# One diffusion block on one core: each engine's instructions ordered by the framework's timeline simulation

## The chip, the cores and the metric

The kernel runs on one core of one Trainium2 chip. The metric is device time of one execution in microseconds (us); less is better. A core has five engines, each with a queue of its own: TensorE (PE) does matmuls and transposes, VectorE (DVE), ScalarE (ACT) and GpSimd (POOL) do elementwise work, and SyncE (SP) issues the DMA transfers of the weights.

## The reference

One layer of a diffusion backbone over 256 latent tokens, with 256 context tokens that only give keys and values. D is 2048, the feed-forward width 8192, all in float32:

```python
mod_l = jnp.split(silu_c @ w_mod[l] + b_mod[l], 6, axis=-1)
mod_c = jnp.split(silu_cc @ w_mod[l] + b_mod[l], 6, axis=-1)
hl = modulate(rms_norm(xl, norm1_g[l]), mod_l[0], mod_l[1])
hc = modulate(rms_norm(xc, norm1_g[l]), mod_c[0], mod_c[1])
zl = hl @ w_in[l] + b_in[l]                       # conv a | sgu u,v | q,k,v | 3 gates
zkv = hc @ w_in[l, :, K_OFF:G_OFF] + b_in[l, K_OFF:G_OFF]
y_na_l = neighbourhood_attention(q, k, v, kc, vc, na_rpb[l])
y_conv = conv_branch(z[..., :2 * CONV_DIM], ...)  # gate, 31 taps over tokens, layer norm, silu, projection
y_sgu = sgu_branch(z[..., 2 * CONV_DIM:Q_OFF], ...)
y_att = y_na @ w_na_out
xl = xl + mod_l[2][:, None, :] * ((g_conv * y_conv + g_sgu * y_sgu + g_att * y_att) @ w_o + b_o)
hl2 = modulate(rms_norm(xl, norm2_g[l]), mod_l[3], mod_l[4])
xl = xl + mod_l[5][:, None, :] * (jnp.square(jax.nn.relu(hl2 @ w1 + b1)) @ w2 + b2)
return rms_norm(xl, final_g)
```

## The kernel before

**Weights.** All weights are streamed once, in tiles of 512 KB (128 x 1024 float32), named raw0, raw1, ... in the order of their loads. `Stream.fetch` issues each load on SP (line 84) into one of 8 buffers. A tile that feeds a matmul is split into a rounded part and a rest: whi on ACT (line 90) and wlo on DVE (line 91), 4 buffers of each. A product is then three matmuls of the parts: lines 172 and 173 with the weights stationary (512 and 256 columns), or lines 178, 179 and 180 with the activations stationary (512 columns each). They accumulate in 4 PSUM banks ("acc"); 4 more ("aux") serve transposes, the modulation products and attention.

**Start and key/value blocks.** The rows of D are worked through in five blocks. For each block, `mod_block` multiplies the conditioning vectors with the tiles of `w_mod` on PE (line 314, "gemv"). These tiles are not split, and the four column groups of the array take one row group each:

```python
                for r in range(rt):
                    g = r0 + r
                    q = g % 4
                    PE.matmul(gb[j][32 * q : 32 * q + 32, :cols], lhsT=cst[:, g], rhs=raw[:, r],
                              start=g < 4, stop=g >= NK - 4, tile_position=(0, 32 * q))
```

Its result is copied by ACT (ge, line 332), transposed by PE (gp, line 335) and reduced by DVE (gv, line 336) to a scale and a shift (m1A, m1B). `rows` then transposes the normalized tokens on PE (hT, line 349) and makes h, the input of all projections, in parts: ACT line 356, DVE lines 358 and 359. `kv_block` multiplies h with the key and value columns of the block: banks k (evacuated by ACT, then DVE line 389, then POOL) and banks vb (DVE line 407). The tokens come from `nat` tiles, those of the context from SP at line 240.

**The other modulation vectors** (`mod_cols`) are made on DVE, one product with each half of a tile (lines 874 and 876, "ga"): two per tile of `w_mod`, 16 for a column. `col_finish` transposes such a column on PE (mcol, line 905), sums it on ACT and puts it in place on DVE (line 910). These tiles are dealt in between the weight tiles of the last key/value block, the projections and the gates.

**After that**: query projection and attention, dealt in steps among the projections of the convolution and gating branches (scores S on PE lines 528 and 529, maximum mx and exponent on DVE lines 530 and 532 and ACT, transposes pT on PE line 551, output o on PE line 562); convolution taps on DVE; the branch projections with their gates; the norm of the convolution branch (`spread`: dg on DVE line 695, crs on PE line 696); the output projection; a second norm (n on line 696, x1T transposes on line 1050); the feed-forward part with `bk` banks; and the last norm.

**Order.** The Python code is written in one sequence, with steps dealt out by small counters. The framework takes this program and puts the instructions of each engine into an order of its own, by a simple model of how long things take. Each engine then executes its list from front to back. Buffers and data dependences are what the code says; semaphore waits follow from them.

## Time and profile before

| | |
|---|---|
| runs | 1778.26, 1782.08, 1789.81 us; median 1782.08 |
| profiled execution | 1788.73 us, span 1786.9 us |
| PE / DVE / ACT / POOL busy | 97% / 75% / 48% / 8% |
| granted TensorE clock, mean | 0.994 |
| DMA | 411.86 MB, 230 GB/s over the span |

A row of a timeline gives the start of an instruction or of a run of equal ones, the time from the first start to the last end, and in brackets how long the engine was idle before it and which instruction released it. Matmuls overlap, so the distance from one start to the next tells what one costs. A list of waits adds the idle times up by what was waited for. Idle time of an engine that nothing waits for costs nothing.

### The profile page before, as it was taken

The numbers are of one execution on the slowest core, as the hardware profiler recorded it, in microseconds if no ns is written. First come the engines' busy times: TensorE is split into PE (matmuls) and PEld (weight loads), VectorE is DVE, ScalarE is ACT, GpSimd is POOL, SyncE is SP. The second block draws the span as 40 slices with busy tenths as digits, with TensorE's granted clock in tenths as the row PEclk, the third lists the DMA queues.
The fourth block names the chain that finished last, engine by engine and source line by source line (L and its number), as shares of the span: only waits on it lengthen the run. The fifth ranks groups of instructions, "written<-read, shape, count | busy, mean of one in ns | idle before, by whom it ended". The sixth has DMA issues, their size and how long they took to land.

```text
span 1786.9 us, 24042 instructions
## 1 busy us (share of the span) xinstructions
PE 1731.8 (97%) x8727; PEld 1422.4 (80%) x8727; DVE 1336.6 (75%) x2099; ACT 862.1 (48%) x1290; POOL 150.9 (8%) x193
## 2 busy tenths in 40 slices
PE   6999898999999999999999999999999999999997
PEld 3667787788888888788878878888888888888886
DVE  4656998799989977898877559746775676666664
ACT  4433345987555444554434446543453445334443
POOL 1221450321000100200010010000000000000000
PEclk9999999999999999999999999999999999999999
DMA  9787788645766668899996567757876775666552
GB/s 322 261 309 263 253 262 262 169 138 173 220 187 199 185 206 284 280 324 337 312 322 221 187 192 257 257 191 239 265 250 196 239 223 189 204 196 187 185 195 83
DMA packets 265688, 411.86 MB, mean 230 GB/s; under 512 B 13182, under 2 KB 126002, under 8 KB 265570
## 3 DMA queue, kind: packets, MB, share of 16 engines
q1 hardware_dynamic: 259410, 391.21, 67.8%
q0 software_dynamic: 5584, 18.07, 3.4%
q8 instruction: 68, 1.11, 0.3%
q10 hardware_dynamic: 576, 1.05, 0.2%
q14 instruction: 50, 0.41, 0.1%
HBM read 408.18 MB, written 2.10 MB: 230 GB/s over the span
## 4 chain that ended last, share of the span: by engine, by line
PE 61%; DVE 14%; issue 11%; DMA 10%; ACT 3%; SPq 1%; POOL 0%; DVEq 0%; POOLq 0%; ACTq 0%
PE bk L172 14%; PE bk L180 10%; PE bk L179 10%; PE bk L178 10%; DMA raw<-in_w_mod_dram 7%; PE bk L173 7%; DVE wlo L91 5%; DVE ga L876 3%; DMA raw<-in_w_in_dram 2%; PE k L172 2%; PE gemv L314 1%; ACT whi L90 1%; PE vb L178 1%; PE vb L180 1%; PE vb L179 1%
## 5 line engine op out<-in xcount | busy, mean ns | idle before, releaser
L90 ACT CAST whi<-raw 128x1024 fp32r<-128x1024 f32 x544 | 570.0, 1050 | 605.6 <-PE bk L180 388.5
L91 DVE TENSOR_TENSOR wlo<-raw,whi 128x1024 fp32r<-128x1024 f32 x544 | 672.3, 1239 | 250.6 <-ACT whi L90 248.3
L172 PE MATMUL bk<-h,whi 128*128 128x512 f32 x1536 | 545.2, 398 | 0.0
L173 PE MATMUL bk<-h,wlo 128*128 128x256 f32 x1536 | 432.0, 282 | 2.7 <-DVE wlo L91 2.5
L172 PEld LDWEIGHTS bk<-h,whi 128*128 128x128 f32 x1536 | 289.6, 189 | 71.0 <-issue 3.1
L173 PEld LDWEIGHTS bk<-h,wlo 128*128 128x128 f32 x1536 | 291.5, 190 | 5.5 <-DVE wlo L91 4.3
L876 DVE SCALAR_TENSOR_TENSOR ga<-raw,cst,ga 128x512 f32<-128x512 f32 x240 | 185.9, 776 | 73.4 <-DMA raw<-in_w_mod_dram 70.5
L179 PE MATMUL bk<-wlo,g 128*128 128x512 f32 x512 | 199.2, 389 | 0.0
L180 PE MATMUL bk<-whi,g 128*128 128x512 f32 x512 | 199.2, 389 | 0.0
L178 PE MATMUL bk<-whi,g 128*128 128x512 f32 x512 | 199.2, 389 | 0.0
L179 PE MATMUL bk<-wlo,h 128*128 128x512 f32 x448 | 175.2, 391 | 3.7 <-DVE wlo L91 3.6
L178 PE MATMUL bk<-whi,h 128*128 128x512 f32 x448 | 175.5, 392 | 0.0
L180 PE MATMUL bk<-whi,h 128*128 128x512 f32 x448 | 174.5, 390 | 0.0
L179 PEld LDWEIGHTS bk<-wlo,g 128*128 128x128 f32 x512 | 96.1, 188 | 20.0
L178 PEld LDWEIGHTS bk<-whi,g 128*128 128x128 f32 x512 | 96.1, 188 | 19.9
L180 PEld LDWEIGHTS bk<-whi,g 128*128 128x128 f32 x512 | 96.1, 188 | 19.9
L637 DVE SCALAR_TENSOR_TENSOR cT<-uT,wcT,cT 128x244 f32<-128x244 f32 (+14 forms) x240 | 107.2, 497 | 0.5
L179 PEld LDWEIGHTS bk<-wlo,h 128*128 128x128 f32 x448 | 84.1, 188 | 23.2 <-DVE wlo L91 6.3
L172 PE MATMUL k<-h,whi 128*128 128x512 f32 x256 | 94.9, 411 | 3.9 <-DVE h L359 2.8
L180 PEld LDWEIGHTS bk<-whi,h 128*128 128x128 f32 x448 | 84.1, 188 | 17.4
L178 PEld LDWEIGHTS bk<-whi,h 128*128 128x128 f32 x448 | 84.1, 188 | 17.2
L173 PE MATMUL k<-h,wlo 128*128 128x256 f32 x256 | 72.6, 285 | 0.5 <-DVE wlo L91 0.5
(267 smaller groups left out, 2075.8 us busy)
## 6 DMA issues: line engine op xcount, KB each, us to landing
raw<-in_w_ff_dram SPq DMA_DIRECT2D x256, 512.0 KB, 4.4
raw<-in_w_in_dram SPq DMA_DIRECT2D x208, 512.0 KB, 4.6
raw<-in_w_mod_dram SPq DMA_DIRECT2D x192, 512.0 KB, 5.2
raw<-in_w_o_dram SPq DMA_DIRECT2D x32, 512.0 KB, 4.4
raw<-in_w_na_out_dram SPq DMA_DIRECT2D x16, 512.0 KB, 3.7
raw<-in_w_sgu_out_dram SPq DMA_DIRECT2D x16, 512.0 KB, 5.4
raw<-in_w_conv_out_dram SPq DMA_DIRECT2D x16, 512.0 KB, 7.2
bias<-in_na_rpb_dram POOLq DMA_DIRECT2D x16, 192.0 KB, 4.8
```

The source lines that it names most:

```text
L90: nc.scalar.copy(hv, rv)
L91: nc.vector.tensor_tensor(lv, rv, hv.bitcast(F32), ALU.subtract)
L172: PE.matmul(bk, lhsT=hi[:, j, c0 : c0 + P], rhs=xhl, start=start, stop=False)
L173: PE.matmul(bk[:, T:], lhsT=lo[:, j, c0 : c0 + P], rhs=xhl[:, :T], start=False, stop=stop)
L178: PE.matmul(bk, lhsT=xh, rhs=hi, start=start, stop=False)
L179: PE.matmul(bk, lhsT=xh, rhs=lo, start=False, stop=False)
L180: PE.matmul(bk, lhsT=xl, rhs=hi, start=False, stop=stop)
L314: PE.matmul(gb[j][32 * q : 32 * q + 32, :cols], lhsT=cst[:, g], rhs=raw[:, r], start=g < 4, stop=g >= NK - 4, tile_position=(0, 32 * q))
L637: V.scalar_tensor_tensor(a[:, lo:hi], u[:, lo + d : hi + d], wj, a[:, lo:hi], ALU.mult, ALU.add)
L876: V.scalar_tensor_tensor(a[0], raw[:, r], sc, a[0], ALU.mult, ALU.add)
```

## The change

The context that the program is built in is told to order the instructions by its timeline simulation in place of its simple model:

```diff
--- before.py
+++ after.py
@@ -1205,7 +1205,7 @@
         arrays[f"in_{name}_dram"] = a
         args.append(nc.dram_tensor(f"in_{name}_dram", a.shape, mybir.dt.from_np(a.dtype), kind="ExternalInput").ap())
     args.append(nc.dram_tensor("out_0_dram", (1, T, D), F32, kind="ExternalOutput").ap())
-    with tile.TileContext(nc) as tc:
+    with tile.TileContext(nc, schedule_with_timeline_sim=True) as tc:
         tile_block(tc, *args)
     r = run_bass_kernel_spmd(nc, [arrays], core_ids=[0])
     return r.results[0]["out_0_dram"]
```

Each engine executes the same instructions as before; their order and a few waits differ. On PE 2468 of 8480 matmuls stand at another place, by at most 184 places, on DVE 1471 of 2089 instructions by at most 119, on ACT 512 by at most 21. Nearly all of them belong to the time up to some 820 us; the feed-forward part stands as it was. On SP 15 loads move, all among the first 33: the context tiles nat_23 and nat_24 go ahead of raw8 and raw9, nat_38 goes behind raw15 and nat_49 behind raw18 (before they stood ahead of raw10 and of raw12). On POOL 17 instructions move by at most 4 places. ACT and DVE follow the moved loads in the order of their first splits.

PE, the modulation product of the second key/value block (gemv_151 with raw34 to raw38; vb_155 is the last value bank of the first block). Before:

```order
L179 MATMUL vb_155_863<-wlo33_819,h_113_612 128x512
L180 MATMUL vb_155_863<-whi33_818,h_113_612 128x512
L314 MATMUL gemv_151_826<-raw34_824,cst_91 32x512 x2
L314 MATMUL gemv_151_826<-raw35_829,cst_91 32x512 x2
L314 MATMUL gemv_151_826<-raw36_833,cst_91 32x512 x2
L314 MATMUL gemv_151_826<-raw37_837,cst_91 32x512 x2
L314 MATMUL gemv_151_826<-raw38_871,cst_91 32x512 x2
L335 MATMUL gp_158_898<-ident_76,ge_157_896 128x128 x4
```

The same in the change, among the key banks k_121 to k_131 of the first block:

```order
L314 MATMUL gemv_151_826<-raw34_824,cst_91 32x512 x2
L172 MATMUL k_121_659<-h_113_612,whi23_562 128x512
L173 MATMUL k_121_659<-h_113_612,wlo23_563 128x256
L172 MATMUL k_125_677<-h_113_612,whi23_562 128x512
L173 MATMUL k_125_677<-h_113_612,wlo23_563 128x256
L314 MATMUL gemv_151_826<-raw35_829,cst_91 32x512 x2
L172 MATMUL k_127_686<-h_108_597,whi23_562 128x512
L173 MATMUL k_127_686<-h_108_597,wlo23_563 128x256
L172 MATMUL k_127_686<-h_108_597,whi23_562 128x512
L173 MATMUL k_127_686<-h_108_597,wlo23_563 128x256
L314 MATMUL gemv_151_826<-raw36_833,cst_91 32x512 x2
```

Ten matmuls that stood next to each other now stand in pairs, each pair between key matmuls.

DVE, the last key/value block (h_316 and h_321 are the last four columns of h; ga_329 and ga_365 two columns of the other modulation vectors). Before:

```order
L358 TENSOR_SCALAR hf_317_2032<-hT_315_2027,m1A_138,m1B_139 128x256
L358 TENSOR_SCALAR hf_319_2039<-hT_318_2035,m1A_138,m1B_139 128x256
L359 TENSOR_TENSOR h_316_2030<-hf_317_2032,h_316_2030 128x256
L359 TENSOR_TENSOR h_316_2030<-hf_319_2039,h_316_2030 128x256
L358 TENSOR_SCALAR hf_322_2047<-hT_320_2042,m1A_138,m1B_139 128x256
L358 TENSOR_SCALAR hf_324_2054<-hT_323_2050,m1A_138,m1B_139 128x256
L359 TENSOR_TENSOR h_321_2045<-hf_322_2047,h_321_2045 128x256
L359 TENSOR_TENSOR h_321_2045<-hf_324_2054,h_321_2045 128x256
```

The end of that piece in the change, and what follows it:

```order
L359 TENSOR_TENSOR h_321_2045<-hf_322_2047,h_321_2045 128x256
L359 TENSOR_TENSOR h_321_2045<-hf_324_2054,h_321_2045 128x256
L876 SCALAR_TENSOR_TENSOR ga_365_2404<-raw112_2402,cst_91,ga_365_2404 128x512
L876 SCALAR_TENSOR_TENSOR ga_329_2123<-raw106_2254,cst_91,ga_329_2123 128x512
L876 SCALAR_TENSOR_TENSOR ga_365_2404<-raw112_2402,cst_91,ga_365_2404 128x512
L876 SCALAR_TENSOR_TENSOR ga_365_2404<-raw113_2407,cst_91,ga_365_2404 128x512 x2
L876 SCALAR_TENSOR_TENSOR ga_365_2404<-raw116_2479,cst_91,ga_365_2404 128x512 x2
L876 SCALAR_TENSOR_TENSOR ga_365_2404<-raw117_2483,cst_91,ga_365_2404 128x512 x2
L389 TENSOR_TENSOR t_333_2158<-k_332_2149,t_333_2158 128x256
```

Products of line 876 stand between the steps that make h and ahead of them, so that these come 14 to 19 places later; the key evacuations of line 389 come after a row of products, 15 to 18 places later.

PE, the same block (mcol_378 is the transposed column ga_365, k_357 a key bank). Before:

```order
L172 MATMUL k_352_2307<-h_321_2045,whi104_2194 128x512
L173 MATMUL k_352_2307<-h_321_2045,wlo104_2195 128x256
L905 MATMUL mcol_354_2332<-ident_76,ga_329_2123 128x128 x4
L172 MATMUL k_357_2350<-h_306_1998,whi107_2260 128x512
L173 MATMUL k_357_2350<-h_306_1998,wlo107_2261 128x256
```

In the change:

```order
L172 MATMUL k_352_2307<-h_321_2045,whi104_2194 128x512
L173 MATMUL k_352_2307<-h_321_2045,wlo104_2195 128x256
L905 MATMUL mcol_378_2629<-ident_76,ga_365_2404 128x128 x4
L172 MATMUL k_357_2350<-h_306_1998,whi107_2260 128x512
L173 MATMUL k_357_2350<-h_306_1998,wlo107_2261 128x256
```

The transposes of ga_329 (mcol_354) and of the convolution weights (line 605) went up, ahead of the bank k_340, and those of ga_365, which stood 161 rows behind k_357, now stand ahead of it.

## Rows read from the trace of the kernel before

**Rows 1.** The page: busy time, share of the span, instructions of each engine.
```profile
PE 1731.8 (97%) x8727; PEld 1422.4 (80%) x8727; DVE 1336.6 (75%) x2099; ACT 862.1 (48%) x1290; POOL 150.9 (8%) x193
```
**Rows 2.** Stages: length; PE, PEld, DVE, ACT, POOL busy; clock, DMA share, GB/s.
```profile
150.00:200.00 50.00, 49.05 (x263) 38.23 (x262) 41.36 (x65) 18.41 (x35) 19.59 (x19) 1.00 0.84 285
200.00:250.00 50.00, 46.06 (x240) 38.60 (x239) 48.36 (x82) 23.65 (x54) 23.65 (x21) 0.97 0.70 224
...
300.00:350.00 50.00, 44.39 (x253) 36.10 (x253) 42.36 (x97) 46.47 (x94) 11.76 (x14) 0.97 0.64 184
...
1110.00:1700.00 590.00, 588.24 (x3003) 500.88 (x3002) 384.11 (x489) 264.23 (x332) 1.59 (x3) 1.00 0.68 217
```
**Rows 3.** Timeline of PE, 14 to 64 us: start, length, instruction, [idle before].
```profile
19.27 1.08 PE L314 MATMUL gemv<-raw,cst 128*32 128x256 f32 x8 [0.42 <-DMA raw<-in_w_mod_dram]
20.86 1.08 PE L314 MATMUL gemv<-raw,cst 128*32 128x256 f32 x8 [0.51 <-DMA raw<-in_w_mod_dram]
...
31.38 0.77 PE L172 MATMUL k<-h,whi 128*128 128x512 f32 x1 [2.79 <-DVE h L359]
```
**Rows 4.** Timeline of PE, groups of line 314 between 64 and 84 us.
```profile
74.23 1.05 PE L314 MATMUL gemv<-raw,cst 128*32 128x512 f32 x2
75.21 0.50 PE L172 MATMUL k<-h,whi 128*128 128x512 f32 x1
...
81.05 1.92 PE L314 MATMUL gemv<-raw,cst 128*32 128x512 f32 x16
82.90 0.50 PE L178 MATMUL vb<-whi,h 128*128 128x512 f32 x1
```
**Rows 5.** Timeline of PE, 206 to 238 us; eight matmuls like the second row.
```profile
206.75 0.90 PE L349 MATMUL hT<-ident,nat 128*128 128x128 f32 x6 [3.64 <-DVE gv L336]
...
207.88 0.63 PE L178 MATMUL vb<-whi,h 128*128 128x512 f32 x1
...
211.10 0.39 PE L180 MATMUL vb<-whi,h 128*128 128x512 f32 x1
...
237.38 0.60 PE L905 MATMUL mcol<-ident,ga 128*128 128x128 f32 x4
237.74 0.48 PE L172 MATMUL k<-h,whi 128*128 128x512 f32 x1
```
**Rows 6.** Timeline of DVE: the last product of raw121.
```profile
257.92 0.74 DVE L876 SCALAR_TENSOR_TENSOR ga<-raw,cst,ga 128x512 f32<-128x512 f32 x1
```
**Rows 7.** DVE's groups by line, 200 to 262 us: busy us, mean ns, idle before.
```profile
L876 DVE SCALAR_TENSOR_TENSOR ga<-raw,cst,ga 128x512 f32<-128x512 f32 x31 | 25.8, 844 | 0.7 <-DMA raw<-in_w_mod_dram 0.6
L91 DVE TENSOR_TENSOR wlo<-raw,whi 128x1024 fp32r<-128x1024 f32 x9 | 14.1, 1564 | 0.7 <-ACT whi L90 0.7
L407 DVE TENSOR_TENSOR vN<-vN,vb 128x512 f32<-128x512 f32 x10 | 6.7, 682 | 0.6 <-PE vb L180 0.6
L389 DVE TENSOR_TENSOR t<-k,t 128x256 f32<-128x256 f32 x16 | 6.5, 415 | 0.1
```
**Rows 8.** What PE waited for, 300 to 450 us: us in total, times, longest.
```profile
PE S L528 <- DVE mx L532: 3.2, 1, 3.2
PE S L529 <- ACT kl L502: 2.0, 2, 1.2
PE o L562 <- DVE mx L532: 1.7, 2, 1.5
```
**Rows 9.** Timeline of PE, late places: the two norms.
```profile
746.03 0.73 PE L696 MATMUL crs<-dg,ones 128*128 128x128 f32 x4 [2.82 <-DVE dg L695]
...
747.31 0.63 PE L180 MATMUL bk<-whi,sg 128*128 128x512 f32 x1
...
1061.63 1.19 PE L696 MATMUL n<-dg,ones 128*128 128x128 f32 x4 [3.88 <-DVE dg L695]
```

## The prediction

> **What bounds the kernel now.** I read the busy shares first, then the stages, then the waits of TensorE (PE), then the timelines of the stages that the change touches. PE is busy for 97% of the span [rows 1]; the page counts matmuls that overlap, so what can be lost or won is the time in which PE starts nothing, and that lies in stages. In the feed-forward part it is near nothing: 588.24 of 590 us are busy [rows 2], and its order stays. VectorE (DVE), 75% on average, is the second limit and a local one: from 200 to 250 us it is busy for 48.36 of 50 us, while in the 50 us before it had 8.6 us to spare [rows 2]. So in the last block of keys and values, whatever is put in front of something that PE needs makes PE late by its own length.
>
> The profiled execution took 1788.73 us (span 1786.9 and 1.8 around it), 6.65 above the median of the three runs, 1782.08. The sum is made against the profiled one and then carried over by taking 6.65 off.
>
> **The change, part by part.** No operation is added or taken away, so every price is one of place: a wait that comes, a wait that goes, and matmuls that run alone where they ran side by side.
>
> *The first loads.* The two first context tiles go ahead of raw8 and raw9, the first two weight tiles of the keys. The matrix-vector matmuls at 19.27 and 20.86 each start when a tile has landed [rows 3], so tiles of 512 KB come some 1.5 us apart, and raw8 comes 2 x 1.5 = 3 us later. PE's first key matmul waits until 31.38 for DVE's h [rows 3]; part of the 3 us falls under that wait. The other two context tiles go behind four and seven modulation tiles, 6 to 10 us later in the queue; they feed the second context rows, which PE needs at some 46 us, with the value matmuls in between as cover. If the cover holds, the price is 0; if both come out, some 5 us. I take +2.5, the middle.
>
> *The matrix-vector rounds.* Four column groups of the modulation product run side by side when their matmuls stand next to each other. A round of two matmuls takes PE from 74.23 to 75.21, 0.98 us; two full rounds of 16 take 81.05 to 82.90, 1.85, so 0.93 each [rows 4]. A round with one or two matmuls thus costs as much as one with eight. Counting neighbours in the order of before gives 43 rounds in 22 groups, in the change 48 in 26, all the extra ones of 512 columns: raw34 to raw38 become five groups among the key matmuls instead of one. Five rounds at 0.93 are 4.65 us; from below it is the two or three that can fall under an idle PE at the start, so 2 us, from above 4.65 with four more entries into a group at 0.3 each, 6 us. I take +4.5, near the full price, because most of the split rounds stand between matmuls that wait for nothing.
>
> *The last key and value block, 201 to 265 us: what goes.* PE waits 3.64 us at 206.75 for DVE's gv, and the eight matmuls after it take 0.63 us where 0.39 is usual [rows 5]: 8 x 0.24 = 1.9. In the change PE does two more value banks before those transposes, so both go: -5.5.
>
> *What comes.* DVE makes h_316 and h_321 14 to 19 places later, behind gate products of line 876, and PE must turn the second gate column, mcol_378, ahead of k_357, where before it stood 161 rows behind k_357. Its products end with raw121, in before at 257.92 + 0.74 = 258.66 [rows 6]. Of what DVE did between 206.5 and 258.7 only a little is moved behind them: 8 key evacuations of line 389, 2 splits of line 91, 3 of line 407 and three small ones, so 8 x 0.415 + 2 x 1.564 + 3 x 0.682 [rows 7] + 1.3 = 9.8 us. Since DVE is full there, the last product ends at 258.7 - 9.8 = 248.9 or so. k_357 started 237.74, right behind the 0.36 us of mcol_354 at 237.38 [rows 5]. It can now start at 248.9 + 0.4 = 249.3, which is 11.6 later; 0.9 of it is transposes that PE did later before and no longer has to. So PE leaves this block about 10.7 us behind, the 5.5 won already in it, and h_316 only moves a part of that wait to an earlier place. The splits that later blocks wait for are late by the same queue.
>
> How does that add to the 7 us of the first two parts? If DVE comes to 206 us in time, the lag at the end is the 10.7 alone, since a late PE waits less for DVE. If DVE is held up as much as PE is, it is 7 + 10.7 = 17.7. DVE had 8.6 us to spare in the 50 us before [rows 2], which speaks for the first; its tiles come through the same raw buffers that PE's lag holds, which speaks for the second. I take 13, so +6 for this block on top of the 7. From below, DVE keeps up and the block gives its 5.5 back.
>
> [...]
>
> *Attention, 297 to 450 us.* PE's scores, transposes and outputs move up to 181 places later in its order, behind projection matmuls that are ready. Three waits, S for DVE's maximum 3.2, S for the low half of the keys 2.0 and o for the maximum 1.7 [rows 8], are 6.9 us, and the slow matmuls after the 3.2 cost about as much as those at 207.88, 1.5 more. That is -8.4 if all go. Nothing is gained if DVE, 42.36 of 50 us busy there [rows 2] and now with the tail of the block before in front, is as late as the scores are; I take -8, since the moves (some 25 matmuls of 0.35 a pair and more) are longer than any of the three waits.
>
> *Late places.* The 2.82 us for crs at 746.03 goes (its transposes are 17 places later) and with it eight matmuls at 0.63 [rows 9], -4.7. Against that, up to 4.5 us of normalization now stands ahead of eleven weight splits in DVE's order at 722 to 737 us, which PE reaches about 3 us late, and one such split at 908 costs 0.7. At 1061.63 PE already waits 3.88 for dg [rows 9]; the second norm product now stands behind eight transposes (1.8 us) and three more of DVE's products come before the first h2, +2 to +3. Together +2; all bad +6, all good -4.
>
> **The sum:** 2.5 + 4.5 + 6 - 8 + 2 = +7, so 1795.7 against the profiled time, and 1789 against the median.
>
> **Rivals.**
> *The DVE queue decides, and nothing gives it back.* The mechanism is the same wait of mcol_378 and k_357, with DVE arriving at 206 us as late as PE: lag 17.7, and the backlog then reaches attention, where its waits stay (0 in place of -8). It decides from the point where DVE's 8.6 us to spare are used up by late tiles. 17.7 + 2 is +19.7, so 1802, slower by just over 1%. For it: the 48.36 of 50 and the small part that moved behind. Against it: the spare time, and attention moved far.
> *DVE keeps up.* The removed waits are real rows and the added ones are only worked out: 2.5 + 4.5 - 5.5 - 8.4 - 4 is -11, so 1771; with the cheap ends of the first two parts, 0 and 2, it is 1766. For it: the products need no PE, and a faster start of the tiles would let them run in idle DVE time. Against it: DVE has hardly any idle time at 200 to 250.
> *The order hardly matters.* PE is the full engine, and a lag in one place is a shorter wait in the next: 1782. The feed-forward half speaks for it, the list of waits against it. [...] The 48.36 of 50 us [rows 2] speaks against it for one stage.
>
> **How the numbers follow.** Forecast, 1789, a chance of 0.57; the DVE queue, 0.23; DVE keeps up, 0.12; no effect, 0.08. One per cent, about what a measurement of this kernel can tell from no change, is 17.8 us, so faster means under 1764 and slower over 1800. Faster needs the second rival with all its cheap ends, and more: 0.09. Slower takes the first rival and the upper edge of the forecast, whose bad ends (+5, +6, +6 in place of 2.5, 4.5 and 2) reach 1797: 0.25. The rest, 0.66, is within. The range, 1769 to 1806, takes in most of the second rival and of the first, a tenth left out at each end.
>
> **What would show it.** In the changed profile: the first key matmul at 33 to 34 us; more and shorter groups of line 314 between 65 and 110; no wait of the transposes for gv near 206, but waits of k for h (line 359) near 222 to 230 and of mcol for ga (line 876) near 245 to 260, together 8 to 15 us; fewer than 3 us of waits for mx, kl and pT in attention; no wait for dg near 746. A list of PE's waits without mcol or h in it would make the largest positive term wrong; waits for mx as long as before would make the largest negative one wrong. A new line in the feed-forward stage would lie outside all of this.

## The result and the profile after

The change makes the kernel slower: 1823.56 us median of 4 runs (1821.57 to 1828.80) against 1781.62 for the kernel before, a ratio of 1.0229 (95% interval 1.0206 to 1.0251). The forecast was 1789, range 1769 to 1806, with a chance of 0.25 for slower by over 1%. The profiled execution took 1821.57 us, span 1819.7, 32.8 us longer than that of before.

PE executes the same matmuls. Its busy time grew by 9.8 of these 32.8 us; the rest is time between matmuls. The page's busy row, which answers to [rows 1]:

```profile
PE 1741.6 (96%) x8727; PEld 1426.9 (78%) x8727; DVE 1328.4 (73%) x2099; ACT 862.0 (47%) x1290; POOL 149.5 (8%) x193
```

Two of the stages, with the columns of [rows 2]. From 200 to 250 us PE is busy for 40.00 us in place of 46.06, and the granted clock is 0.90 in place of 0.97; DVE is as full as before:

```profile
200.00:250.00 50.00, 40.00 (x198) 33.01 (x198) 48.51 (x82) 15.62 (x34) 14.82 (x15) 0.90 0.83 262
...
300.00:350.00 50.00, 46.05 (x261) 38.87 (x260) 43.29 (x89) 36.51 (x72) 5.15 (x6) 0.97 0.73 225
```

What PE waited for over the whole span of the changed kernel (us in total, times, longest). The waits for gv, crs, kl and o of before are gone, as forecast. In their place stand waits for h, for weight splits (wlo), for m and for nat:

```profile
PE bk L179 <- DVE wlo L91: 9.3, 7, 3.6
PE k L172 <- DVE h L359: 9.2, 3, 8.1
...
PE mT L853 <- DVE m L843: 6.3, 1, 6.3
PE hT L349 <- ACT nat L262: 5.0, 1, 5.0
PE bk L173 <- DVE wlo L91: 4.7, 6, 1.2
PE n L696 <- DVE dg L695: 3.9, 1, 3.9
PE S L528 <- DVE mx L532: 3.7, 2, 2.9
```

Where each of them stands, from PE's timeline of the changed kernel (start, length, instruction, idle before); these rows answer to [rows 3, 5, 9]:

```profile
49.06 1.11 PE L349 MATMUL hT<-ident,nat 128*128 128x128 f32 x4 [4.99 <-ACT nat L262]
...
234.80 0.76 PE L172 MATMUL k<-h,whi 128*128 128x512 f32 x1 [8.07 <-DVE h L359]
...
242.87 0.60 PE L905 MATMUL mcol<-ident,ga 128*128 128x128 f32 x4
...
256.55 0.60 PE L905 MATMUL mcol<-ident,ga 128*128 128x128 f32 x4
...
741.18 0.50 PE L179 MATMUL bk<-wlo,h 128*128 128x512 f32 x1 [3.56 <-DVE wlo L91]
...
775.58 0.50 PE L179 MATMUL bk<-wlo,h 128*128 128x512 f32 x1 [1.85 <-DVE wlo L91]
...
785.99 0.64 PE L179 MATMUL bk<-wlo,h 128*128 128x512 f32 x1 [2.23 <-DVE wlo L91]
...
932.51 2.36 PE L853 MATMUL mT<-ident,m 128*128 128x128 f32 x8 [6.25 <-DVE m L843]
...
1093.80 0.79 PE L172 MATMUL bk<-h,whi 128*128 128x512 f32 x1 [2.57 <-DVE h L1084]
```

The two mcol rows carry no wait, although the forecast put the wait of the last key and value block there; it stands at 234.80, before a key matmul that needs h.

Behind each of these waits the matmuls are slower for a while. From 229.8 to 240.1 us, a stretch that begins within the wait of 8.07 us, the granted clock is 0.50, and a key pair (lines 172 and 173) comes every 0.64 us, where later it comes every 0.36:

```profile
235.57 0.63 PE L172 MATMUL k<-h,whi 128*128 128x512 f32 x1
...
236.21 0.63 PE L172 MATMUL k<-h,whi 128*128 128x512 f32 x1
...
244.50 0.40 PE L172 MATMUL k<-h,whi 128*128 128x512 f32 x1
...
244.86 0.40 PE L172 MATMUL k<-h,whi 128*128 128x512 f32 x1
```

The eight pairs from 234.80 to 240.05 cost 2.4 us more for it. The clock is 0.50 behind the waits at 49.06, 741.18, 775.58, 785.99, 932.51 and 1093.80 too, for 3.4 us from 741.83, for 6.8 from 929.57. After the first 47 us PE is busy for 30 us at a clock of 0.50, in the profile before for 16; an estimate from the pairs is that this makes 6 of the 32.8 us.

There are eight places at which every engine has finished the same set of instructions in both orders. They cut the program into pieces, and for each piece the time at which PE ends its matmuls can be compared. The table gives what PE lost in each (us, changed profile less profile before; the same for the experiments below). Pieces that a run leaves as they were differ from the profile before by -3 to +3, and the first piece by about -2, since that one profile of before started slowly (eight rows of line 314 take 1.08 us there [rows 3], at 19.56 us of the changed profile 0.64).

| kernel | 0-47 | 47-199 | 199-297 | 297-670 | 670-790 | 790-1005 | 1005-1120 | rest |
|---|---|---|---|---|---|---|---|---|
| forecast | +2.5 | +4.5 | +6 | -8 | -2 | +1 | +3 | 0 |
| the change | 3.2 | 5.4 | 10.6 | -5.8 | 8.1 | 6.0 | 1.4 | 2.6 |
| e1 loads only | 3.4 | 0.8 | 0.6 | -0.1 | -1.8 | -1.7 | 1.3 | 3.0 |
| e2 rounds only | -1.8 | 5.1 | -0.3 | -0.5 | 0.5 | -1.9 | -1.3 | -0.5 |
| e3 kv only | -1.7 | -1.4 | 10.1 | -2.0 | 1.3 | -0.1 | -0.4 | 1.5 |
| e4 attention only | -2.1 | 0.1 | -0.4 | -4.5 | -1.8 | -1.2 | 0.1 | -1.7 |
| e5 mid only | -3.1 | -0.3 | -0.3 | -1.2 | 7.4 | -1.1 | -1.2 | -1.9 |
| e6 gate only | -1.9 | -0.3 | -1.3 | 0.4 | -2.1 | 5.9 | -1.3 | -0.8 |
| e9 norm, ff only | -1.2 | -0.8 | -0.4 | -0.3 | 0.5 | -1.9 | 1.5 | 3.4 |

So the first three pieces cost 19.2 where 13 was forecast, attention gave back 5.8 where 8 was, and the pieces after 670 us cost 18.1 where 2 was. The table places 31.5 of the 41.9 us between the medians; most of the rest is that the profiled execution of before was 7.1 us above its median and that of the change 2.0 below.

### The profile page after: what moved, and what is told of

Read it like the earlier page. It is cut to its first block, busy times and chain, and to the rows that moved or that the text cites. A ratio compares the mean times of both kernels' runs of the same rounds, so it can differ in the third digit from the quotient of the medians.

```text
span 1819.7 us, 24048 instructions
## 1 busy us (share of the span) xinstructions
PE 1741.6 (96%) x8727; PEld 1426.9 (78%) x8727; DVE 1328.4 (73%) x2099; ACT 862.0 (47%) x1290; POOL 149.5 (8%) x193
## 4 chain that ended last, share of the span: by engine, by line
PE 57%; DMA 14%; DVE 13%; issue 11%; ACT 3%; SPq 1%; POOL 0%; DVEq 0%; POOLq 0%; ACTq 0%
PE bk L172 14%; DMA raw<-in_w_mod_dram 13%; PE bk L179 9%; PE bk L180 9%; PE bk L178 9%; PE bk L173 7%; DVE wlo L91 4%; DVE ga L876 4%; PE gemv L314 2%; PE k L172 2%; PE k L173 1%; ACT whi L90 1%; PE vb L178 1%; PE vb L180 1%; PE vb L179 1%
## 5 line engine op out<-in xcount | busy, mean ns | idle before, releaser
L637 DVE SCALAR_TENSOR_TENSOR cT<-uT,wcT,cT 128x255 f32<-128x255 f32 (+14 forms) x240 | 110.7, 497 | 0.1
L178 PEld LDWEIGHTS bk<-whi,h 128*128 128x128 f32 x448 | 85.3, 191 | 18.1
L172 PEld LDWEIGHTS k<-h,whi 128*128 128x128 f32 x256 | 49.9, 197 | 41.4 <-issue 12.6
```

The costliest lines, as they stand in the source:

```text
L172: PE.matmul(bk, lhsT=hi[:, j, c0 : c0 + P], rhs=xhl, start=start, stop=False)
L178: PE.matmul(bk, lhsT=xh, rhs=hi, start=start, stop=False)
L637: V.scalar_tensor_tensor(a[:, lo:hi], u[:, lo + d : hi + d], wj, a[:, lo:hi], ALU.mult, ALU.add)
```

## Experiments

**How an order is held.** All kernels are the kernel before with a table of instruction numbers for each engine and edges that keep each engine to it. Nothing else is changed unless it is said. No run holds the whole order of before in this way; the pieces that a run leaves as they were, -3 to +3 in the table, stand in for it.

```diff
+def hold(tc):
+    here = {i.name: i for i in tc.nc.cur_bb.bb.instructions}
+    for row in zlib.decompress(base64.b85decode("".join(ORDER))).decode().split(";"):
+        names = [f"I-{n}" for n in itertools.accumulate(map(int, row.split(",")))]
+        names = [n for n in names if n in here]
+        for a, b in zip(names, names[1:]):
+            tc.add_manual_dep(here[b], a, mybir.DependencyInfo(mybir.DependencyClass.NoSync, ...), reason="order")
...
     with tile.TileContext(nc) as tc:
         tile_block(tc, *args)
+        hold(tc)
```

**One piece at a time.** In e1, e2, e3, e4, e5, e6 and e9 the table has the order of the change in one piece of the program and the order of before in all others.

e1, the first loads:

> Every engine keeps the order of before, except its first piece, up to 46.6 us of the profile of before (105 PE matmuls, 55 DVE instructions, the first 34 loads), which has the order of the change. The prediction gave this piece +2.5 us. In the changed profile PE ends these 105 matmuls 3.2 us later than before (50.0 against 46.8). Theory 'own price' (each piece costs by its own order what its stage showed): PE 3.2 us behind at the end of the piece and still 3.2 behind at the end, 1785 on the median. Rival 'absorbed' (a late PE waits less for DVE further on): at most 1 us is left after 210 us, where before has a wait of 3.6 us for gv.

Measured: 1791.75 us, ratio 1.0050 (1.0033 to 1.0067). With the slow start of the profile of before taken off, the piece costs some 5.5, and nothing is absorbed at 206 us. The medians differ by 9.1; the other 3.6 are placed in no piece that this run changes (its feed-forward part, with the order of before, lost 3.0). PE's first transposes of the second context rows waited for nat; ACT's timeline of the changed kernel shows why. The last context tile, which went seven loads back on SP, comes at 46.27:

```profile
46.27 0.63 ACT L250 ACTIVATE sq<-nat 128x512 f32<-128x512 f32 x1 [5.14 <-DMA nat<-in_ctx_dram]
```

e2, the matrix-vector rounds:

> The order of before everywhere, except the piece from 46.6 to 199 us, in which the modulation products (line 314) stand in 48 rounds in place of 43. The prediction gave it +4.5 us (five rounds at 0.93). Theory 'own price': PE is 5.4 us behind at 199 us, as in the changed profile (8.6 there less 3.2 from the first piece), and the end is 5 us later, 1787. Rival 'absorbed': the lag shrinks to under 2 at 297 us, since DVE is then ahead of PE and the 3.6 us wait for gv near 206 is spent while PE still works.

Measured: 1788.27 us, ratio 1.0031 (1.0018 to 1.0044). 5.1 us behind over the piece, and still there at 297 us. In the changed profile the split groups stand on PE like this, 1.88 apart with two key pairs in between; they answer to [rows 4]. The trace has two rows for each matmul of line 314 (320 for the 160 of the program), so x4 is two matmuls, half a round of four, and takes the 0.98 us of a round:

```profile
80.13 1.05 PE L314 MATMUL gemv<-raw,cst 128*32 128x512 f32 x4
...
82.01 1.05 PE L314 MATMUL gemv<-raw,cst 128*32 128x512 f32 x4
...
83.88 1.05 PE L314 MATMUL gemv<-raw,cst 128*32 128x512 f32 x4
```

e3, the last key and value block:

> The order of before everywhere, except the piece from 199 to 297 us (last key and value block, 485 PE matmuls, 137 DVE instructions). The prediction: the block alone leaves PE 10.7 us behind, and when PE comes late from earlier stages only 6 are added. Theory 'DVE as late as PE' (the rival on record with 1802): +10.6 alone, the same as it added in the changed profile (19.2 less 8.6), so 1792. Theory 'spare time': alone it is +10.7 too, but in the sum it should have been 6, so the first two pieces must have held DVE up as well. Rival 'carried lag': alone the block costs 5 or less, since DVE is on time when PE is, and the 8.1 us wait for h shrinks to under 4.

Measured: 1794.09 us, ratio 1.0059 (1.0041 to 1.0078), 10.1 us over the piece. With PE on time the wait for h at the same matmul is as long as in the whole change, 8.1 us; so it does not come from a lag carried in. From PE's waits, 190 to 300 us:

```profile
PE k L172 <- DVE h L359: 8.4, 2, 8.1
PE k L172 <- DVE t L389: 2.5, 4, 0.8
```

e4, attention:

> The order of before everywhere, except the piece from 297 to 670 us (attention, taps, projections of the conv and gating branches). The prediction: -8.4, all three waits gone (mx 3.2, kl 2.0, mx for o 1.7) and 1.5 of slow matmuls. The changed profile shows the lag fall from 19.2 to 13.4 over this piece, -5.8, with 3.7 us of waits for mx left. Theory 'own price': -6, 1776. Theory 'backlog' (the waits left in the changed profile come from a DVE that is late from the block before): alone it is -8 or better, under 1 us of waits for mx, 1774.

Measured: 1779.04 us, ratio 0.9983 (0.9971 to 0.9994), -4.5 over the piece. Theory "backlog" fails: with DVE on time one wait for mx stays and is 4.4 us, at 301 us, the only wait in the list from 290 to 470 us:

```profile
PE S L528 <- DVE mx L532: 4.4, 1, 4.4
```

e5, 670 to 790 us:

> The order of before everywhere, except the piece from 670 to 790 us (norm of the convolution branch, first gate steps; 507 PE matmuls, 148 DVE instructions). The prediction gave its parts -4.7 and +3, so about -2. In the changed profile PE falls 8.1 us back over this piece: waits of 3.2, 2.0 and 1.9 for splits that stand in DVE's order behind a product of line 876 whose tile has not landed, or behind eight steps of the norm. Theory 'head of the line' (the order of these rows makes the wait, whatever went before): +8 alone, so 1790, with the same three waits for wlo. Rival 'out of step' (loads and DVE are late relative to PE because of the 13 us lag carried in): +2 or less alone, waits under 1 us each.

Measured: 1789.74 us, ratio 1.0039 (1.0025 to 1.0054), 7.4 us over the piece. "Head of the line" holds: PE waited for splits 9 times from 660 to 1060 us, 13.6 us in all, in the profile before 5 times and 4.3.

e6, 790 to 1005 us:

> The order of before everywhere, except the piece from 790 to 1005 us (gates of the last branch; 942 PE matmuls, 208 DVE instructions). The prediction gave it +0.7. In the changed profile it costs 6.0: PE's transposes mT wait 6.3 us for DVE's m, which stands behind one product of line 876 on raw394; that tile was issued at 919.06 and landed at 931.0. Theory 'head of the line': +6 alone, 1788.5, one wait of 4 to 7 us for m. Rival 'out of step': +1 or less, since in the profile of before DVE stood 4.0 us before the same product, with m already done.

Measured: 1789.41 us, ratio 1.0048 (1.0028 to 1.0068), 5.9 us over the piece, with one wait of 7.1 us for m.

e9, the second norm and the feed-forward part:

> The order of before everywhere, except the last piece, from 1005 us to the end (second norm, feed-forward part; on PE only 260 rows near the norms move, on DVE neighbours change places). The prediction: +2 to +3 at the second norm and nothing in the feed-forward part. In the changed profile PE falls back 1.4 us at the norm and 2.6 in the feed-forward part, where four splits are waited for (1.2 at most). Theory 'own price': +4, 1786.5. Rival 'chance' (the feed-forward waits come and go from run to run): +1.5 at the norm and between -1 and +2 after it, 1784.

Measured: 1793.10 us, ratio 1.0056 (1.0040 to 1.0071). The norm costs 1.5. The feed-forward part showed 3.4, with five waits for splits; but e1, whose feed-forward order is that of before, lost 3.0 there, so this piece is not settled, and the medians differ by 8.9, which is 4 us more than the two pieces of its one profile show. From PE's waits of this run, 1110 us to the end:

```profile
PE bk L173 <- DVE wlo L91: 3.9, 5, 1.1
```

The seven pieces alone sum to 9.1 + 5.6 + 11.4 - 3.6 + 5.4 + 5.0 + 8.9 = 41.8 us (median of each less the median of before in the same runs). The whole change measured 1823.56 - 1781.62 = 41.9. Each of the seven is known to 2 to 4 us, so their sum to some 8, and the close agreement is in part luck, since e1 and e9 are some 4 us longer by their medians than by their pieces. In the traces the changed pieces alone sum to 32.3, and the whole change to 31.5. So the pieces add; an absorption of several us is not excluded.

**Why the late pieces lose.** The changed DVE timeline around m: a product of line 876 at the head of DVE's queue waits 6.54 us for its tile (raw394, issued 919.06, landed 931.0), and m, whose operands had been ready since 924.6, stands behind it:

```profile
923.29 1.27 DVE L842 SCALAR_TENSOR_TENSOR th<-th,bk 128x512 f32<-128x512 f32 x2
931.11 0.75 DVE L876 SCALAR_TENSOR_TENSOR ga<-raw,cst,ga 128x512 f32<-128x512 f32 x1 [6.54 <-DMA raw<-in_w_mod_dram]
931.77 1.28 DVE L843 TENSOR_TENSOR m<-m,th 128x512 f32<-128x512 f32 x2
```

In the profile before DVE waited at the same product too, but with m already made:

```profile
901.25 0.68 DVE L843 TENSOR_TENSOR m<-m,th 128x512 f32<-128x512 f32 x1
905.90 0.75 DVE L876 SCALAR_TENSOR_TENSOR ga<-raw,cst,ga 128x512 f32<-128x512 f32 x1 [3.97 <-DMA raw<-in_w_mod_dram]
```

The same at 735 us: a split that PE needs, wlo283, stands behind a product that waits 1.51 us for its tile, eight norm steps and another product:

```profile
735.39 0.75 DVE L876 SCALAR_TENSOR_TENSOR ga<-raw,cst,ga 128x512 f32<-128x512 f32 x1 [1.51 <-DMA raw<-in_w_mod_dram]
736.06 2.74 DVE L656 SCALAR_TENSOR_TENSOR cT<-cmean,cT 128x256 f32<-128x256 f32 x8
738.71 0.75 DVE L876 SCALAR_TENSOR_TENSOR ga<-raw,cst,ga 128x512 f32<-128x512 f32 x1
739.37 3.43 DVE L91 TENSOR_TENSOR wlo<-raw,whi 128x1024 fp32r<-128x1024 f32 x2
```

e7 takes three rows out of these places and leaves the rest of the change. On DVE:

```diff
-product on raw394; m; m; wlo387
+m; m; wlo387; product on raw394
...
-product on raw309; wlo302
+wlo302; product on raw309
...
-product on raw291; 8 norm steps; product on raw291; wlo283
+wlo283; product on raw291; 8 norm steps; product on raw291
```

> The whole order of the change, except three instructions on DVE: the product on raw394 goes behind m and one weight split (near 931 us of the changed profile), the product on raw309 behind the split wlo302 (774 us), and the split wlo283 ahead of the product on raw291 and the eight norm steps (735 us). Theory 'head of the line': the waits of 6.3 for m, 2.0 for wlo302 and 3.2 for wlo283 go, -10 to -12, so 1812 to 1814. Rival 'out of step': the tiles and buffers hold PE up at the next instruction, -3 or less, 1821.

Measured: 1818.59 us, ratio to before 1.0201 (1.0174 to 1.0228), 5 us faster than the whole change; -3.5 and -1.7 in the two pieces. The intervals of the two ratios overlap a little, so the reading rests on the pieces as well. Between the two theories: the wait for m is gone, and 4.4 of its 6.3 us come back one step later, since the product still waits and now wlo388 stands behind it. DVE's row of e7 for that product, and PE's waits from 920 to 935 us:

```profile
930.17 1.54 DVE L876 SCALAR_TENSOR_TENSOR ga<-raw,cst,ga 128x512 f32<-128x512 f32 x2 [5.32 <-DMA raw<-in_w_mod_dram]
```
```profile
PE bk L179 <- DVE wlo L91: 4.4, 1, 4.4
```

e12 asks why the tile is late. It is e6 with one line more:

```diff
-            GP.dma_start(xb[cb], x[0][:, cb * 512 : (cb + 1) * 512].rearrange("(t p) n -> p t n", p=P))
+            GP.memset(xb[cb], 0.5)
```

> As gate_only (the order of before, with the piece from 790 to 1005 us in the order of the change), but the four residual tiles xb, 512 KB each, are filled by POOL with a constant in place of four transfers, so that the residual input is left out. In gate_only DVE stands before the product on raw394, with m behind it, and PE waits 7.1 us for m; the four transfers go on the DMA engines in that stretch (median 9.0 us to landing). Theory 'slow tile': raw394 comes late because the xb transfers share the DMA engines; without them the wait for m is under 1.5 us and PE loses under 1 us over the piece in place of 5.9. Rival 'late buffer': raw394 is late because its buffer comes free late; the wait for m stays above 5.

Measured: 1784.39 us (one run), 2.1 us over the piece in place of 5.9; the wait for m fell from 7.1 to 2.4, that of DVE before the product from 8.32 to 3.75. So the four transfers are the larger part of the tile's lateness and not the whole of it. DVE's row in e6 and the same in e12:

```profile
904.36 0.75 DVE L876 SCALAR_TENSOR_TENSOR ga<-raw,cst,ga 128x512 f32<-128x512 f32 x1 [8.32 <-DMA raw<-in_w_mod_dram]
```
```profile
902.56 0.75 DVE L876 SCALAR_TENSOR_TENSOR ga<-raw,cst,ga 128x512 f32<-128x512 f32 x1 [3.75 <-DMA raw<-in_w_mod_dram]
```

**Why the key and value block loses.** e8 moves eight rows of DVE's table in the whole change, lines 358 and 359 of h_316 and h_321, to directly behind h_311:

```diff
-h_311; product; vN; 2 products; 2 splits; ...; 4 hf; ...; 4 h
+h_311; 4 hf; 4 h; product; vN; 2 products; 2 splits; ...
```

> The whole order of the change, except eight instructions on DVE: the last four columns of h (h_316 and h_321, lines 358 and 359) go directly behind h_311, ahead of the products. The prediction: DVE is full in this block, so PE only waits at another place, for the products of mcol; the block still costs 10 (wait for h under 2, waits for mcol or k 6 to 8), the total stays within 3 of 1823. Rival 'head of the line': the 8.1 us wait for h falls and nothing takes its place, -7, 1816.

Measured: 1823.53 us, ratio to before 1.0228 (1.0200 to 1.0256), the same as the whole change. The waits for h fell from 9.2 to 1.9, those for key evacuations grew from 1.8 to 5.6, and all waits of the block fell from 12.4 to 10.2. Still the block cost 12.1, in place of 10.6: the granted clock from 200 to 250 us is 0.82, in the whole change 0.90, so more of its matmuls ran slowly: with its waits in between, its key pairs come about 0.64 us apart from 229.58 to 241.43 and from 247.53 to 252.18, in the whole change from 234.80 to 240.05. From PE's waits of e8, 200 to 320 us:

```profile
PE k L172 <- DVE t L389: 5.6, 2, 3.8
PE k L172 <- DVE h L359: 1.9, 2, 1.6
```

e10 is e3 with less work in each product, e13 the whole change with the same edit:

```diff
-                        V.scalar_tensor_tensor(a[0], raw[:, r], sc, a[0], ALU.mult, ALU.add)
+                        V.scalar_tensor_tensor(a[0][:, :128], raw[:, r, :128], sc, a[0][:, :128], ALU.mult, ALU.add)
```

> The order of before with the last key and value block (199 to 297 us) in the order of the change, as in the run kv_only, but every product of line 876 works on 128 of its 512 columns, so that three quarters of these modulation vectors are left out. This takes load off DVE and changes neither the order nor the loads. Theory 'DVE is full' (the block costs what the products in front take on DVE): the wait for h falls from 8.1 to under 3, and nothing replaces it; PE loses under 4 us over the block in place of 10. Rival 'waits for loads' (the products stand before tiles that have not landed): the wait for h stays at 6 or more, since an early product still waits for its tile.

> The whole order of the change, with every product of line 876 on 128 of 512 columns, so that three quarters of these modulation vectors are left out; to be held against quarter_products, which has the order of before outside the last key and value block. Theory 'two mechanisms': the block at 199 to 297 us costs under 4 (DVE's load), but PE still waits for m near 920 us (5 or more) and for splits near 740 and 780 us (together 4 or more), since a short product waits for its tile as long as a full one; the first two pieces still cost 7 to 9. Rival 'DVE's load is all': the losses at 670 to 790 and 790 to 1005 us fall under 2 each.

Measured, one run each: 1771.01 and 1796.32 us. What PE lost in each piece:

| kernel | 0-47 | 47-199 | 199-297 | 297-670 | 670-790 | 790-1005 |
|---|---|---|---|---|---|---|
| e10 | -0.4 | -1.6 | 1.6 | -5.0 | -5.1 | -4.6 |
| e13 | 3.3 | 4.8 | 1.9 | -9.2 | 2.9 | 1.6 |

The block falls from 10 to under 2 in both: with this order, most of its time is DVE's load. How much of the fall the order of before would show too is open, since no run has it with short products, and e10 gains 4.6 to 5.1 us in each of the three pieces behind, which have the order of before. The wait for h came out between the two theories, at 5.1: PE passes that matmul at 219.70, 3.5 us earlier than in e3, and comes to it 0.5 earlier. From 670 to 1005 us e13 loses 8.0 and 6.2 more than e10, as much as the whole change lost with full products (8.1 and 6.0). So the length of the products changes nothing there; DVE stands and waits for tiles. The norm steps among them keep their length in e13, and what they add from 670 to 790 us is not separated. PE's waits of e13, 800 to 1010 us and 660 to 800 us:

```profile
PE mT L853 <- DVE m L843: 5.3, 1, 5.3
```
```profile
PE bk L179 <- DVE wlo L91: 5.7, 4, 2.7
```

**Moving PE's rows and not DVE's.** e11 and e14 keep DVE, ACT and the loads in the order of before outside attention:

```diff
-hT_308 ... hT_323 among the matmuls of vb_325 and vb_326
+hT_308 ... hT_313 behind 4 matmuls of vb_326, hT_315 ... hT_323 each one matmul later
...
-S_411 behind 4 matmuls of bk_402 and bk_403
+S_411 27 places later
...
-crs ahead of 16 matmuls of bk_763 and bk_764
+crs 17 places later
```

> The order of before with the attention piece (297 to 670 us) of the change, and four moves on PE alone, each putting a step that waits behind matmuls that are ready, by as many as fill the wait: the transposes hT for gv (206 us, 18 to 23 places later), the scores S_411 of the attention piece (301 us, 27 places), the transposes crs at 746 us (17 places). DVE, ACT and the loads stay as they were. Theory 'PE's order is free where DVE's is not': the waits of 3.6 (hT), 4.4 (S) and 2.8 (crs) and the slow matmuls after each go, -10 to -14 in all with the -3.6 of the attention piece, 1770. Rival 'DVE sets the pace': the time comes back as waits for splits, k banks or scores further on, -4 or less, 1779.

Measured: 1780.66 us, ratio 0.9980 (0.9970 to 0.9991), no better than e4. Of the waits that were filled, 2.4, 2.0 and 3.5 us came up one step later. They stood before rows of PE that could move as well. Two of them, from PE's timeline of e11:

```profile
208.18 0.69 PE L349 MATMUL hT<-ident,nat 128*128 128x128 f32 x2 [2.42 <-DVE hf L358]
...
759.19 1.11 PE L905 MATMUL mcol<-ident,ga 128*128 128x128 f32 x4 [3.53 <-DVE ga L876]
```

e14 moves these too:

```diff
-hT_315 ... hT_323 in the first half of vb_326
+hT_315 ... hT_323 between the first matmuls of vb_327
...
-mcol_779 ahead of bk_772 on whi307
+mcol_779 17 places later
...
-pT_417, one transpose, seven places ahead of the others
+pT_417, all transposes together
```

> As the run best, with three more moves on PE alone: the last four pairs of transposes hT go another 11 to 13 places back (a wait of 2.4 us for hf at 208 us), the transposes mcol_779 17 places back (a wait of 3.5 us for ga at 759 us), the first transpose of pT_417 next to its fellows (2.0 us at 307 us). Theory 'PE's order is free': these three waits go as well, -6 to -8 against the run best, 1774. Rival 'DVE sets the pace': they come back as waits further on, within 2 of 1781.

Measured: 1775.58 us, ratio to before 0.9958 (0.9945 to 0.9972). The whole interval lies below 1, and this version is faster than both kernels, than the one before by 0.4%. The three waits together are down to 1.5 us (0.6 for hf, 0.9 for s from ACT, and no row for ga); -5 against e11 where -6 to -8 was expected. So PE's order is free where the matmuls put in between need nothing new, as far as these runs go.

## Why the prediction was wrong, step by step

- **The first loads**, +2.5, ends 0 and 5: some 5.5 by the trace of e1. The cover, the value matmuls of the first block, did not hold. The upper end was the right one: the last context tile came at 46.27 and PE waited 4.99 us. The other part, a later raw8, did not show: the first key matmul came at 30.22 us, not at 33 to 34.
- **The rounds**, +4.5, ends 2 and 6: 5.1 alone, 5.4 in the change. Right, near the full price of five rounds with their entries. The counts of two, eight and sixteen matmuls in the working are rows, two for each matmul; the price of a round does not change by that.
- **The key and value block, alone** 10.7: 10.1 (e3). The size was right, and so, as far as e8 and e10 go, was the reason, that DVE is full; the place was not. mcol never waited. PE was held at h and at key evacuations ahead of it, and then no longer came early to mcol. The sum left out the slower matmuls behind a new wait (a granted clock of 0.50 from 229.8 to 240.1 us, 2.4 us here), though it counted 1.9, 1.5 and 1.9 us of such matmuls as gains where a wait goes; that the size came out even so is in part luck.
- **How it adds.** This step failed: "I take 13" for the first three parts, between 10.7 and 17.7, on the ground that a late PE waits less for DVE. PE was 19.2 behind at 297 us, and in e1 and e2 a lag of about 5 stayed whole. The 8.6 us to spare in the 50 us before [rows 2] bought nothing. A reading that no run isolates is that with a late PE its hT, its banks and the buffers it gives back are late too, and DVE with them. The rival on record, "DVE arrives as late as PE", was right in this.
- **Attention**, -8: -5.8, and -4.5 alone. Of the three waits of [rows 8] those for kl and o went. The largest stayed, at the same score matmul, the fourth of line 528: 3.18 us before, 2.90 in the change, 4.43 in e4. For this one it failed that the moves are longer than the wait; in e11, 27 places later, it is gone.
- **Late places**, "together +2", ends -4 and +6: this is the step that failed most, with 15.5. The gain at crs came (no wait for dg near 746). Against it the sum priced splits behind 4.5 us of norm steps by their busy time alone, and m not at all, since it looked for work put in front and not for waits put in front. A product of line 876 that stood before its tile had landed held what was behind it on DVE: 6 us at 790 to 1005 and, together with the norm steps in the same places, 8 at 670 to 790, the same with a quarter of the products' work (e13). In the profile before DVE already stood idle for 70.5 us over the span before such products, at raw394 with nothing right behind that PE needed. The row was in the page (line 876, the idle time before it and its releaser), and it was read as idle time of an engine that is not the bottleneck.
- **The feed-forward part**, 0: 2.6, not settled, since e1 lost 3.0 there with the order of before.
- **A new order on DVE.** DVE's rows at 923.29 and 931.77 show m, ready at 924.6, not passing the product that waited 6.54 us for its tile. The rival on record that the order hardly matters did not hold: the whole change is 41.9 us slower by the medians, and in e7, where DVE's order alone differs from the whole change, three rows made 3.5 and 1.7 us in two pieces.

Of the signs that were to show the steps, those for the groups of line 314, for h near 222 to 230 (8.1 us, ending at 234.80), for gv and for dg came out; those for the first key matmul (30.22), for mcol and for attention (4.0 us of waits for mx and s, not under 3) did not.

## What to carry to other kernels

Where the trace shows an engine keep to its order, as DVE did here with m, ready at 924.6 and begun at 931.77, read an instruction's idle time before it as a price on everything behind it: before a step is moved up, ask whether its input has landed, not only how long it runs. The lags of this pipeline, whose engines give each other buffers, added up (32.3 us from the pieces alone, 31.5 in the whole change); count on a later stage to absorb one only where a run shows it. Price a new wait with the slower matmuls behind it (2.4 us behind the wait of 8.07 us here), as one that goes. To fill a wait of the full engine, move that engine's own waiting row behind work that is ready, and follow the wait to the next row before calling it gone.

## What was not expected of the hardware

A 512 KB tile that lands some 5 us after its issue elsewhere (median 5.3 for the w_mod tiles in that stretch of the changed kernel) took 12 us, 919.06 to 931.0, while four transfers of the same size from POOL's queue were under way; with those left out DVE's wait for the tile fell from 8.32 us (e6) to 3.75 (e12). The DMA issues of the changed kernel, 900 to 935 us (count, KB each, median us from issue to landing):

```profile
raw<-in_w_mod_dram SPq DMA_DIRECT2D x6, 512.0 KB, 5.3
xb<-in_x_dram POOLq DMA_DIRECT2D x4, 512.0 KB, 9.0
```
